# Fewer seven-product chunks in a decoder layer's FFN blocks, and accumulators copied out of PSUM by ScalarE at a block's end

## The chip, the cores and the metric

The kernel runs on one core of a Trainium2 chip. Its time is in device microseconds (us), and lower is better. TensorE (PE in the profile) multiplies, VectorE (DVE) and ScalarE (ACT) work elementwise, GpSimd (POOL) does almost nothing here, and SyncE (SP) issues the weight loads. Each of these engines executes its own instructions in its own fixed order and waits for the others by semaphores.

## The reference: what is computed

One decoder layer over 256 tokens of width 2048, in float32: an FFN, a mixer (attention and a recurrent branch), and a second FFN, each followed by a layer norm. The change concerns the two FFNs, which have the same form:

```python
D_MODEL = 2048
SEQ = 256
D_FF = (8 * D_MODEL // 3 + 255) // 256 * 256      # 5632

def swiglu(h, w_in, w_out):
    a, b = jnp.split(h @ w_in, 2, axis=-1)
    return (jax.nn.silu(a) * b) @ w_out

h = layer_norm(DN_ALPHA * h + 0.5 * swiglu(h, ffn1_w_in[l], ffn1_w_out[l]), ln1_g[l], ln1_b[l])
...
h = layer_norm(DN_ALPHA * h + 0.5 * swiglu(h, ffn2_w_in[l], ffn2_w_out[l]), ln3_g[l], ln3_b[l])
```

## The kernel before

**Precision.** A float32 operand is split into a high part (`h`, rounded to fp32r) and a low part (`l`, the rest), and a product is made of three matmuls, high by high, high by low, low by high (`three`, L563 to L566). The activations are the stationary operand and the weights the moving one. So every weight piece that comes from memory has to be split on the chip: ScalarE copies it to the high part `wh` (L192), VectorE subtracts that from the piece to get the low part `wl` (L193).

**Blocks.** `w_in` is worked through in 22 blocks. A block makes 256 columns of `a` and 256 columns of `b` for both halves of the tokens (t = 0 and 1, 128 each), summed over K = 2048. K is cut into four chunks of 512 (four rows of 128).

- A *plain* chunk consists of two pieces of 128x1024, `c` in the plan. Each piece brings 12 matmuls of 512 columns (2 rows x 2 token halves x 3), 24 in a chunk. They accumulate into two PSUM banks, `c[0]` for the first token half and `c[1]` for the second, each with `a` in its left 256 columns and `b` in its right ones. These banks come from the pool `mm`, which has two buffers (`CB`).
- A *seven-product* chunk replaces the eight half-size products of a 2x2 by 2x2 block product with seven (Winograd's form). It has four pieces named by the products they feed: `p1q3` and `q5p7` and `q4p6` with 1024 columns, `p2` with 512. Each product is 6 matmuls of 256 columns, 42 in a chunk. The products p1, p6, p7 and q5 gather in two banks `e` of the pool `bp` (four buffers); the others go straight into `c`. VectorE must first form sums of weights: `ws` (L165, 128x1024) and two of 128x512 (L169, L172).

**Filling work.** The product with `w_out` does not wait for all blocks. A block's plan holds pieces `o` (`fill`), each of which is 12 matmuls of 512 columns into two banks of the pool `ob`, made of gated results of an earlier group of blocks.

**The order on TensorE** is written out by hand by `block_plan(fast, fills, lead)`: `fast` chunks go by seven products, `fills` pieces `o` are spread between, `lead` of them at the very start. Before the change the plans are, after the first two blocks: two pairs of `block_plan(2, 2, 0)` and `block_plan(3, 2)`, then sixteen late blocks `block_plan(3, 4)`. Word for word, the plans that matter run:

```
(2, 2, 0)  c0 p1q3 p2 c2 q5p7 o q4p6 c8 p1q3 p2 o q5p7 c10 q4p6
(3, 2)     o o c0 p1q3 p2 q5p7 q4p6 p1q3 p2 c2 q5p7 q4p6 p1q3 p2 q5p7 q4p6
(2, 2)     o o c0 p1q3 p2 c2 q5p7 q4p6 c8 p1q3 p2 c10 q5p7 q4p6
(3, 4)     o o c0 p1q3 p2 q5p7 o q4p6 p1q3 p2 c2 q5p7 q4p6 p1q3 o p2 q5p7 q4p6
(2, 4)     o o c0 p1q3 p2 o q5p7 c2 q4p6 o p1q3 p2 c8 q5p7 c10 q4p6
```

A block with `lead` 0 thus begins at once with a plain piece, and the others have two pieces `o` ahead of it.

**Pieces ahead.** `Weights.unit` hands out a piece and, before that, has the piece four places ahead split (`AHEAD` = 4) and the one eight places ahead loaded. The split parts `wh` and `wl` have five buffers each (`HL_BUFS`), so a piece can only be split once TensorE has finished the piece five places before it.

**The gate.** When a block is done, `gate` (L853 on) combines `c` and `e` into `a` and `b`, applies Silu to `a` and multiplies. For a block with seven-product chunks ScalarE copies p1 (L859), VectorE makes six operations (L860, L861, L862, twice L865, and the product L871) and ScalarE the Silu (L866). The two operations L865 are the only readers of the banks `c`, and they stand behind the other sums. Seven pieces later (four for the last block) TensorE transposes the result (L877) and it is split again (L689, L690). The order of ScalarE's and VectorE's instructions is not written by hand: a scheduler places the gate's operations between the splits of the next pieces.

**After the last block** `out_product` multiplies the last group of gated results with the rest of `w_out`; its first bank comes from the same pool `mm`.

Of the kernel before, what the change touches and what calls it, by code (L numbers as in the profile page):

```python
# [8 lines left out]
F32 = mybir.dt.float32  # L9
F32R = mybir.dt.float32r  # L10
I32 = mybir.dt.int32
AF = mybir.ActivationFunctionType
OP = mybir.AluOpType
AX = mybir.AxisListType.X

P = 128
S = 256
# [36 lines left out]
Z_BUFS = 1  # L54
# [12 lines left out]
def block_plan(fast, fills, lead=2):  # L67

    chunks = {0: (), 2: (1, 3), 3: (1, 2, 3)}[fast]
    plain = [("c", k) for q in range(4) if q not in chunks for k in (4 * q, 4 * q + 2)]
    forms = [(f, q) for q in chunks for f in FORMS]
    rest = ["o"] * fills
    plan = [(rest.pop(), 0) for _ in range(min(lead, fills))] + [plain.pop(0)]
    slow = []
    while plain or rest:
        for which in (rest, plain) if lead else (plain, rest):
            if which:  # L80
                p = which.pop(0)
                slow.append((p, 0) if p == "o" else p)
    if not forms:
        return plan + slow
    step = len(forms) / (len(slow) + 1)
    n = 0
    for i, f in enumerate(forms):
        plan.append(f)
        if len(slow) > n and i + 1 >= (n + 1) * step:
            plan.append(slow[n])  # L90
            n += 1
    return plan


def layer_plans(first):
    return ([block_plan(0, 0), block_plan(first, 0)] + [block_plan(2, 2, 0), block_plan(3, 2)] * 2
            + [block_plan(3, 4)] * 16)


FILLS = [(g, nb, 2 * p) for g, (b0, b1) in enumerate(SEGS[:-1]) for nb in range(4) for p in range(b1 - b0)]  # L100
# [161 lines left out]
def tile_layer(ctx, tc, x_fm, x_tm, pos, f1a, f1o, wA, wki, wB, lru, wab, wrb, wo, f2a, f2o,  # L262
# [5 lines left out]
    V, A, T, G = nc.vector, nc.scalar, nc.tensor, nc.gpsimd  # L268
    count = [0]

    def name(s):
        count[0] += 1
        return f"{s}{count[0]}"
# [65 lines left out]
    for i in range(NR + LAG):  # L339
        if i < NR:  # L340
            plain([wB[RX + i], wB[RG + i]])
        if i >= LAG:
            g, c = divmod(i - LAG, TPG)
# [8 lines left out]
    W = Weights(nc, pool, pieces, bg.step)  # L352
# [498 lines left out]
    def ffn(x, forms, ln, plans):  # L851
        def gate(c, e, g, i, lag):

            z = W.fast_pool.tile([P, 4 * S], F32, name=name("z"), tag="z", bufs=Z_BUFS)
            z4 = z.rearrange("p (j c) -> p j c", j=4)
            a, b = z4[:, 0:4:2], z4[:, 1:4:2]
            if e:
                p1, p6, p7, q5 = e[0][:, :S], e[0][:, S:], e[1][:, :S], e[1][:, S:]
                A.activation(z4[:, 0], p1, AF.Copy)  # L859
                V.tensor_tensor(z4[:, 1], z4[:, 0], p6, op=OP.add)  # L860
                V.tensor_tensor(z4[:, 2], z4[:, 1], p7, op=OP.add)  # L861
                V.tensor_tensor(b, q5[:, None, :].to_broadcast([P, 2, S]), z4[:, 1:3], op=OP.subtract)  # L862
                for t in range(2):
                    zt = z[:, t * 512:(t + 1) * 512]
                    V.tensor_tensor(zt, zt, c[t], op=OP.add)  # L865
                A.activation(a, a, AF.Silu)  # L866
            else:
                for t in range(2):
                    A.activation(z4[:, 2 * t], c[t][:, :S], AF.Silu)
                    A.activation(z4[:, 2 * t + 1], c[t][:, S:], AF.Copy)  # L870
            V.tensor_tensor(a, a, b, op=OP.mult)  # L871
            for _ in range(lag):
                yield
            ps = BP()
            for k in range(2):
                for t in range(2):
                    T.transpose(ps[:, k * S + t * P:k * S + (t + 1) * P], z[:, t * 512 + k * P:t * 512 + (k + 1) * P], ident)  # L877
            for k in range(2):
                hl = UHL("g")
                split(hl, ps[:, k * S:(k + 1) * S])  # L880
                g[i + k] = hl

        g = [[None] * (2 * (b1 - b0)) for b0, b1 in SEGS]
        fills = deque(FILLS)
        open_ps = []

        def seed():
            s, nb, _ = fills[0]
            open_ps[:] = OB(), OB()

        def fill():
            if not open_ps:
                seed()
            s, nb, k0 = fills.popleft()
            for k in (k0, k0 + 1):
                w = W.unit(512)
                for t in range(2):
                    tokens(open_ps[t], g[s][k], t, w, k == 0, k == len(g[s]) - 1)
            if k0 + 2 == len(g[s]):
                for t in range(2):  # L900
                    y_add(open_ps, nb, False, t)
                if fills:
                    seed()

        for s, (b0, b1) in enumerate(SEGS):
            for n in range(b0, b1):
                c, e = blockF(x, forms, plans[n], fill)
                task = gate(c, e, g[s], 2 * (n - b0), LAG_T[n == NBK - 1])
                next(task)
                bg.add("gate", task)  # L910
        new_stats()
        ln.prepare()
        if not ln.last:
            bg.add("main", later(consts(), W.last.ins))
        out_product(g[-1], ln)
# [239 lines left out]
    for j in range(NR + LAG):  # L1155
# [14 lines left out]
        if j >= LAG:  # L1170
            i = j - LAG
            g, c = divmod(i, TPG)
# [6 lines left out]
            r, t = T1(), T1()  # L1179
# [114 lines left out]
```

## Time and profile before

| | |
|---|---|
| time, median of 3 runs (lowest to highest) | 2427.51 us (2427.35 to 2430.88) |
| the profiled execution: its time | 2428.93 us |
| the profiled execution: its span, first to last instruction | 2427.0 us |
| mean granted TensorE clock | 0.987 |
| busy time of PE, DVE, ACT | 2313.7 us, 2038.9 us, 1410.3 us |
| first FFN's late blocks | about 181 to 686 us |
| second FFN's late blocks | about 1857 to 2362 us |

A row of the time line reads: start, duration, engine, line, operation, output and inputs by the names in the program, shapes, and in brackets how long the engine had sat idle before and what ended that. Matmuls overlap: one of 512 columns is shown as 0.38 us long, though the next begins after some 0.22 us. So an idle time, which is counted from a shown end, is a little shorter than the gap in the stream. A wait for several semaphores is put down to the one that came last by the profile, which need not be the one that the instruction needed.

### The profile page before, as it was taken

To read this page: it belongs to the slowest core of one execution; us is meant where nothing else is said; L and a number is where in the kernel's file an instruction comes from. 1 tells how busy PE (TensorE), PEld (TensorE's weight loads), DVE (VectorE), ACT (ScalarE), POOL (GpSimd) and SP (SyncE) were. 2 spreads that over 40 slices of the span, in tenths; PEclk is the share of its full clock that TensorE was granted. 3 is DMA by queue.
4 is the path that set the end of the run, shared out by engine and by line. 5 is a ranking of instruction groups with operands and counts; after the bars stand their busy time and mean duration, and the time that the engine had idled before them with its cause. 6 is when DMAs were issued, how large, how long until landed. Compare 5 with 4: busy or idle time off the path is not lost.

```text
span 2427.0 us, 37550 instructions
## 1 busy us (share of the span) xinstructions
PE 2313.7 (95%) x14592; PEld 2104.2 (87%) x14592; DVE 2038.9 (84%) x2835; ACT 1410.3 (58%) x1931; POOL 25.9 (1%) x58
## 2 busy tenths in 40 slices
PE   7889999999989999999999999999989999999997
PEld 6788888888878888888999988888878888888886
DVE  7889999999987776655788875666989999999996
ACT  6555655655646555544688874444755655655652
POOL 0000000000000000000000000000000000000001
PEclk9999999999999999999999999999999999999998
DMA  7445555555556554455555555556645555556563
GB/s 285 167 171 195 208 198 197 193 193 194 197 178 213 180 177 156 148 183 189 176 190 183 182 198 185 187 192 194 213 172 203 193 189 199 197 207 222 208 215 111
DMA packets 112770, 463.41 MB, mean 191 GB/s; under 512 B 12720, under 2 KB 12720, under 8 KB 97488
## 3 DMA queue, kind: packets, MB, share of 16 engines
q1 hardware_dynamic: 110592, 454.61, 53.6%
q0 software_dynamic: 2000, 6.41, 1.0%
q8 instruction: 114, 1.87, 0.3%
q14 instruction: 64, 0.52, 0.1%
HBM read 458.87 MB, written 2.10 MB: 190 GB/s over the span
## 4 chain that ended last, share of the span: by engine, by line
PE 83%; DVE 8%; issue 5%; ACT 3%; DMA 1%; POOL 0%; DVEq 0%; SPq 0%; ACTq 0%; POOLq 0%
PE mm L564 8%; PE mm L566 8%; PE mm L565 8%; PE ob L564 6%; PE ob L566 6%; PE ob L565 6%; PE mm L553 5%; PE ob L553 5%; PE bp L566 4%; PE bp L565 4%; PE bp L564 4%; DVE wl L193 3%; PE mm L554 3%; PE ob L554 3%; ACT wh L192 2%
## 5 line engine op out<-in xcount | busy, mean ns | idle before, releaser
L193 DVE TENSOR_TENSOR wl<-raw,wh 128x1024 fp32r<-128x1024 f32 (+3 forms) x630 | 752.7, 1202 | 300.8 <-ACT wh L192 300.3
L192 ACT ACTIVATE wh<-raw 128x1024 fp32r<-128x1024 f32 (+3 forms) x630 | 652.8, 1045 | 502.7 <-issue 146.3
L192 ACT ACTIVATE wh<-rf 128x1024 fp32r<-128x1024 f32 x354 | 320.5, 916 | 181.6 <-PE mm L566 143.9
L193 DVE TENSOR_TENSOR wl<-rf,wh 128x1024 fp32r<-128x1024 f32 x354 | 365.9, 1041 | 10.6 <-ACT wh L192 7.0
L564 PE MATMUL ob<-wh,g 128*128 128x512 f32 x640 | 246.6, 385 | 1.0 <-ACT g L689 1.0
L566 PE MATMUL ob<-wh,g 128*128 128x512 f32 x640 | 243.2, 380 | 0.6 <-DVE g L690 0.6
L565 PE MATMUL ob<-wl,g 128*128 128x512 f32 x640 | 243.1, 380 | 0.0
L564 PE MATMUL mm<-wh,hs 128*128 128x512 f32 (+1 forms) x600 | 207.5, 346 | 30.0 <-ACT wh L192 15.7
L192 ACT ACTIVATE wh<-ws 128x1024 fp32r<-128x1024 f32 x118 | 125.3, 1061 | 146.2 <-issue 62.9
L566 PE MATMUL mm<-wh,hs 128*128 128x512 f32 (+1 forms) x600 | 205.0, 342 | 1.7 <-DVE hs L755 1.4
L565 PE MATMUL mm<-wl,hs 128*128 128x512 f32 (+1 forms) x600 | 204.6, 341 | 0.0
L564 PE MATMUL mm<-wh,xs 128*128 128x256 f32 (+1 forms) x464 | 156.6, 338 | 46.2 <-ACT wh L192 24.5
L565 PE MATMUL bp<-wl,sh 128*128 128x256 f32 x708 | 195.1, 276 | 1.6 <-DVE wl L193 1.6
L566 PE MATMUL bp<-wh,sl 128*128 128x256 f32 x708 | 194.7, 275 | 0.0
L564 PE MATMUL bp<-wh,sh 128*128 128x256 f32 x708 | 194.6, 275 | 0.0
L564 PEld LDWEIGHTS mm<-wh,hs 128*128 128x128 f32 x600 | 114.6, 191 | 48.3 <-ACT wh L192 22.6
L565 PE MATMUL mm<-wl,xs 128*128 128x256 f32 (+1 forms) x464 | 154.2, 332 | 1.3 <-DVE wl L193 1.3
L193 DVE TENSOR_TENSOR wl<-ws,wh 128x1024 fp32r<-128x1024 f32 x118 | 144.0, 1221 | 13.1 <-ACT wh L192 13.1
L566 PE MATMUL mm<-wh,xs 128*128 128x256 f32 (+1 forms) x464 | 154.2, 332 | 0.0
L165 DVE TENSOR_TENSOR ws<-rf 128x1024 f32<-128x1024 f32 x118 | 143.8, 1219 | 0.0
L564 PEld LDWEIGHTS mm<-wh,xs 128*128 128x128 f32 x464 | 90.4, 195 | 60.6 <-ACT wh L192 30.5
L565 PEld LDWEIGHTS bp<-wl,sh 128*128 128x128 f32 x708 | 135.8, 192 | 3.6 <-DVE wl L193 2.4
(301 smaller groups left out, 5795.3 us busy)
## 6 DMA issues: line engine op xcount, KB each, us to landing
raw<-wB SPq DMA_DIRECT2D x144, 512.0 KB, 3.6
rf<-f1a SPq DMA_DIRECT2D x60, 1024.0 KB, 4.8
rf<-f2a SPq DMA_DIRECT2D x58, 1024.0 KB, 4.9
raw<-f1o SPq DMA_DIRECT2D x88, 512.0 KB, 5.7
raw<-f2o SPq DMA_DIRECT2D x88, 512.0 KB, 5.7
raw<-wA SPq DMA_DIRECT2D x64, 512.0 KB, 3.6
raw<-f2a SPq DMA_DIRECT2D x60, 512.0 KB, 4.9
raw<-f1a SPq DMA_DIRECT2D x56, 512.0 KB, 5.7
```

Of the source, the lines that this page charges most:

```text
L165: v.tensor_tensor(t, b[:, 0:4:3], b[:, 1:2].to_broadcast([P, 2, 2, 256]), op=OP.add)
L192: nc.scalar.activation(hp, src, AF.Copy)
L193: self.last = nc.vector.tensor_tensor(lp, src, hp, op=OP.subtract)
L553: T.matmul(ps, w[0], x.rearrange("p a t -> p (a t)"), start=first, stop=False)
L554: T.matmul(ps[:, :S], w[1], x[:, 0], start=False, stop=last)
L564: T.matmul(ps, xh, h, start=start, stop=False, skip_group_check=seeded)
L565: T.matmul(ps, xh, l, start=False, stop=False, skip_group_check=seeded)
L566: T.matmul(ps, xl, h, start=False, stop=stop, skip_group_check=seeded)
```

## The change

Two edits, in `layer_plans` and in `gate`.

1. The plans. The second block of each early pair goes from `block_plan(3, 2)` to `block_plan(2, 2)`; of the sixteen late blocks every second one goes from `block_plan(3, 4)` to `block_plan(2, 4)`, so that late blocks alternate between three and two seven-product chunks. In each FFN that is 2 + 8 = 10 chunks which become plain.
2. The gate. The tile `z` grows from four to six parts of 256 columns. ScalarE copies each bank `c[t]` to SBUF in one instruction (L860, `a` into part 0 or 2, `b` into part 4 or 5), then p1 (L861). VectorE works on with the copies: L862 to L867 and the product, now L873. The Silu is L868.

```diff
 def layer_plans(first):
-    return ([block_plan(0, 0), block_plan(first, 0)] + [block_plan(2, 2, 0), block_plan(3, 2)] * 2
-            + [block_plan(3, 4)] * 16)
+    return ([block_plan(0, 0), block_plan(first, 0)] + [block_plan(2, 2, 0), block_plan(2, 2)] * 2
+            + [block_plan(3, 4), block_plan(2, 4)] * 8)
...
-            z = W.fast_pool.tile([P, 4 * S], F32, name=name("z"), tag="z", bufs=Z_BUFS)
-            z4 = z.rearrange("p (j c) -> p j c", j=4)
-            a, b = z4[:, 0:4:2], z4[:, 1:4:2]
+            z = W.fast_pool.tile([P, 6 * S], F32, name=name("z"), tag="z", bufs=Z_BUFS)
+            z6 = z.rearrange("p (j c) -> p j c", j=6)
+            a, b = z6[:, 0:4:2], z6[:, 1:4:2]
             if e:
                 p1, p6, p7, q5 = e[0][:, :S], e[0][:, S:], e[1][:, :S], e[1][:, S:]
-                A.activation(z4[:, 0], p1, AF.Copy)
-                V.tensor_tensor(z4[:, 1], z4[:, 0], p6, op=OP.add)
-                V.tensor_tensor(z4[:, 2], z4[:, 1], p7, op=OP.add)
-                V.tensor_tensor(b, q5[:, None, :].to_broadcast([P, 2, S]), z4[:, 1:3], op=OP.subtract)
                 for t in range(2):
-                    zt = z[:, t * 512:(t + 1) * 512]
-                    V.tensor_tensor(zt, zt, c[t], op=OP.add)
+                    A.activation(z6[:, 2 * t:5 + t:4 - t], c[t].rearrange("p (j c) -> p j c", j=2), AF.Copy)
+                A.activation(z6[:, 1], p1, AF.Copy)
+                V.tensor_tensor(z6[:, 0], z6[:, 0], p1, op=OP.add)
+                V.tensor_tensor(z6[:, 1], z6[:, 1], p6, op=OP.add)
+                V.tensor_tensor(z6[:, 3], z6[:, 1], p7, op=OP.add)
+                V.tensor_tensor(z6[:, 2], z6[:, 2], z6[:, 3], op=OP.add)
+                V.tensor_tensor(b, q5[:, None, :].to_broadcast([P, 2, S]), b, op=OP.subtract)
+                V.tensor_tensor(b, b, z6[:, 4:6], op=OP.add)
                 A.activation(a, a, AF.Silu)
```

How the scheduler places the new operations is shown at three places. The numbers behind the names count buffers; `mm` are the banks `c`, `bp` the banks `e`, `raw`, `rf` and `ws` the unsplit pieces, and `wh` with a number is the piece of that number.

On ScalarE, at the end of the first FFN's thirteenth block, a late one (its gate is the tile z173), before. The pieces 208 and 209 are the third and fourth of the following block.

```order
L192 ACTIVATE wh208_4023<-raw208_3954 128x1024
L192 ACTIVATE wh209_4039<-rf209_3973 128x1024
L859 ACTIVATE z173_4057<-bp166_3794 128x256
L192 ACTIVATE wh210_4068<-rf209_3973 128x512
L192 ACTIVATE wh211_4085<-ws209_4041 128x1024
L192 ACTIVATE wh212_4106<-raw212_4021 128x1024
L866 ACTIVATE z173_4057<-z173_4057 128x2x256
```

The same place after; the pieces 198 and 199 are here the third and fourth of the following block.

```order
L192 ACTIVATE wh197_3906<-raw197_3828 128x1024
L192 ACTIVATE wh198_3916<-raw198_3847 128x1024
L860 ACTIVATE z173_3952<-mm164_3667 128x2x256
L192 ACTIVATE wh199_3934<-rf199_3866 128x1024
L860 ACTIVATE z173_3952<-mm165_3668 128x2x256
L861 ACTIVATE z173_3952<-bp166_3687 128x256
L192 ACTIVATE wh200_3964<-rf199_3866 128x512
L192 ACTIVATE wh201_3983<-raw201_3904 128x1024
L868 ACTIVATE z173_3952<-z173_3952 128x2x256
```

The copy of the first bank now stands ahead of the split of the next block's fourth piece, that of the second bank right behind it, and the Silu two splits after the copy of p1 where it was three.

On VectorE, the same gate before.

```order
L860 TENSOR_TENSOR z173_4057<-z173_4057,bp166_3794 128x256
L169 TENSOR_TENSOR rf209_3973<-ws209_4041,rf209_3973 128x2x256
L861 TENSOR_TENSOR z173_4057<-z173_4057,bp167_3795 128x256
L193 TENSOR_TENSOR wl210_4069<-rf209_3973,wh210_4068 128x512
L862 TENSOR_TENSOR z173_4057<-bp167_3795,z173_4057 128x2x256
L172 TENSOR_TENSOR rf209_3973<-rf209_3973 128x2x256
L865 TENSOR_TENSOR z173_4057<-z173_4057,mm164_3774 128x512
L865 TENSOR_TENSOR z173_4057<-z173_4057,mm165_3775 128x512
L193 TENSOR_TENSOR wl211_4086<-ws209_4041,wh211_4085 128x1024
L871 TENSOR_TENSOR z173_4057<-z173_4057 128x2x256
```

And after.

```order
L862 TENSOR_TENSOR z173_3952<-z173_3952,bp166_3687 128x256
L863 TENSOR_TENSOR z173_3952<-z173_3952,bp166_3687 128x256
L169 TENSOR_TENSOR rf199_3866<-ws199_3936,rf199_3866 128x2x256
L864 TENSOR_TENSOR z173_3952<-z173_3952,bp167_3688 128x256
L193 TENSOR_TENSOR wl200_3965<-rf199_3866,wh200_3964 128x512
L865 TENSOR_TENSOR z173_3952<-z173_3952 128x256
L193 TENSOR_TENSOR wl201_3984<-raw201_3904,wh201_3983 128x1024
L866 TENSOR_TENSOR z173_3952<-bp167_3688,z173_3952 128x2x256
L172 TENSOR_TENSOR rf199_3866<-rf199_3866 128x2x256
L867 TENSOR_TENSOR z173_3952<-z173_3952 128x2x256
L193 TENSOR_TENSOR wl202_4004<-ws199_3936,wh202_4003 128x1024
L873 TENSOR_TENSOR z173_3952<-z173_3952 128x2x256
```

No operation of VectorE reads a bank `mm` any more, and the gate's operations lie between three splits where they lay between two.

On ScalarE at the end of the first FFN's fourth block (gate z83), behind which a block with `lead` 0 begins, before.

```order
L192 ACTIVATE wh52_1171<-rf51_1087 128x512
L192 ACTIVATE wh53_1190<-raw53_1123 128x1024
L859 ACTIVATE z83_1206<-bp78_980 128x256
L192 ACTIVATE wh54_1219<-ws51_1161 128x1024
L866 ACTIVATE z83_1206<-z83_1206 128x2x256
L192 ACTIVATE wh55_1238<-raw55_1157 128x1024
```

And after.

```order
L860 ACTIVATE z83_1184<-mm76_969 128x2x256
L192 ACTIVATE wh50_1149<-rf49_1066 128x512
L192 ACTIVATE wh51_1168<-raw51_1101 128x1024
L860 ACTIVATE z83_1184<-mm77_970 128x2x256
L861 ACTIVATE z83_1184<-bp78_988 128x256
L192 ACTIVATE wh52_1200<-ws49_1133 128x1024
L192 ACTIVATE wh53_1219<-raw53_1129 128x1024
L192 ACTIVATE wh54_1237<-rf49_1066 128x1024
L868 ACTIVATE z83_1184<-z83_1184 128x2x256
L192 ACTIVATE wh55_1247<-raw55_1166 128x1024
```

The Silu, which needs results of VectorE, stood one split behind the copy of p1 and now stands three behind it.

More of the change, by code (lines that the diff above doesn't have):

```diff
@@ L868, in gate @@
                 for t in range(2):
-                    A.activation(z4[:, 2 * t], c[t][:, :S], AF.Silu)
-                    A.activation(z4[:, 2 * t + 1], c[t][:, S:], AF.Copy)
+                    A.activation(z6[:, 2 * t], c[t][:, :S], AF.Silu)
+                    A.activation(z6[:, 2 * t + 1], c[t][:, S:], AF.Copy)
             V.tensor_tensor(a, a, b, op=OP.mult)
```

## Prediction

> **What bounds the kernel now.** I read the page first, for the busy time by slices.
>
> ```profile
> PE 2313.7 (95%) x14592; PEld 2104.2 (87%) x14592; DVE 2038.9 (84%) x2835; ACT 1410.3 (58%) x1931; POOL 25.9 (1%) x58
> PE   7889999999989999999999999999989999999997
> DVE  7889999999987776655788875666989999999996
> ```
>
> TensorE looks full everywhere; VectorE is full in the first and last third alone, which are the two FFNs. The windows tell the two apart there: thirteen late blocks of the first FFN, from one gate to another (start and end are the two copies of p1 below), and a stretch of two early blocks.
>
> ```profile
> 246.28:654.60 408.32, 393.71 (x2627) 364.07 (x2626) 402.45 (x482) 243.98 (x287) 0.00 (x0) 1.00 0.54 201
> 66.12:118.38 52.26, 51.92 (x338) 48.09 (x338) 44.53 (x54) 29.48 (x36) 0.00 (x0) 0.97 0.45 162
> 246.28 0.39 ACT L859 ACTIVATE z<-bp 128x256 f32<-128x256 f32 x1 [0.28 <-PE bp L566]
> 654.60 0.38 ACT L859 ACTIVATE z<-bp 128x256 f32<-128x256 f32 x1 [0.28 <-PE bp L566]
> ```
>
> A late block takes 408.32 / 13 = 31.41 us. VectorE is busy for 402.45 / 13 = 30.96 us of it (98.6%), TensorE for 30.29. So in the late blocks VectorE sets the pace. In the early stretch VectorE is busy for only 85% and TensorE hardly waits (0.34 us in 52).
>
> Where TensorE loses its time is seen in its time line and VectorE's, around one block's end.
>
> ```profile
> 403.35 0.38 PE L565 MATMUL ob<-wl,g 128*128 128x512 f32 x1
> 408.10 0.38 PE L566 MATMUL ob<-wh,g 128*128 128x512 f32 x1
> 409.62 0.45 PE L564 MATMUL mm<-wh,xs 128*128 128x512 f32 x1 [1.14 <-ACT wh L192]
> 409.91 0.38 PE L565 MATMUL mm<-wl,xs 128*128 128x512 f32 x1
> 408.79 1.28 DVE L865 TENSOR_TENSOR z<-z,mm 128x512 f32<-128x512 f32 x2
> 408.52 1.06 ACT L192 ACTIVATE wh<-raw 128x1024 fp32r<-128x1024 f32 x1 [1.53 <-PE ob L566]
> ```
>
> The profile blames a split, but that is the wrong name: in ScalarE's order the split at 408.52 is wh212, and the first plain piece that TensorE starts at 409.62 is wh208, four splits earlier. What ends just before 409.62 is the first of the two operations L865 (begun at 408.79, some 0.6 us each), which frees the bank `c[0]`. TensorE waits for VectorE's gate. The other such waits:
>
> ```profile
> 66.12 0.77 PE L564 MATMUL mm<-wh,xs 128*128 128x512 f32 x1 [7.52 <-DVE z L865]
> 127.68 0.77 PE L564 MATMUL mm<-wh,xs 128*128 128x512 f32 x1 [9.03 <-DVE z L865]
> 188.05 0.45 PE L564 MATMUL mm<-wh,xs 128*128 128x512 f32 x1 [2.72 <-DVE z L865]
> 221.14 0.45 PE L564 MATMUL mm<-wh,xs 128*128 128x512 f32 x1 [1.12 <-ACT wh L192]
> 690.74 0.76 PE L564 MATMUL mm<-wh,g 128*128 128x512 f32 x1 [4.78 <-DVE z L865]
> 1803.23 0.77 PE L564 MATMUL mm<-wh,hs 128*128 128x512 f32 x1 [9.03 <-DVE z L865]
> 1863.79 0.45 PE L564 MATMUL mm<-wh,hs 128*128 128x512 f32 x1 [2.71 <-DVE z L865]
> 2366.59 0.77 PE L564 MATMUL mm<-wh,g 128*128 128x512 f32 x1 [3.46 <-DVE z L865]
> ```
>
> The row at 221.14 stands for 30: fifteen in each FFN, one a late block, 1.11 to 1.27 us each. The long ones stand where a block with `lead` 0 follows, and behind the last block.
>
> **The change part by part.**
>
> *Matmuls: a loss.* The page counts the seven-product chunks by their loads: 60 and 58. After the change there are 50 and 48.
>
> ```profile
> rf<-f1a SPq DMA_DIRECT2D x60, 1024.0 KB, 4.8
> rf<-f2a SPq DMA_DIRECT2D x58, 1024.0 KB, 4.9
> 412.28 0.27 PE L564 MATMUL bp<-wh,xs 128*128 128x256 f32 x1
> 415.52 0.28 PE L566 MATMUL bp<-wh,sl 128*128 128x256 f32 x1
> ```
>
> From 403.35 to 408.10 lie 22 steps of 512 columns, 0.216 us each; from 412.28 to 415.52 lie 29 steps of 256, 0.1117 us each. A plain chunk costs 24 x 0.216 = 5.18 us, one by seven products 42 x 0.1117 = 4.69 us. Twenty chunks cost TensorE 20 x 0.49 = **9.8 us** more. [...]
>
> *VectorE: relief.*
>
> ```profile
> 402.32 2.35 DVE L193 TENSOR_TENSOR wl<-raw,wh 128x1024 fp32r<-128x1024 f32 x2
> 404.59 1.22 DVE L193 TENSOR_TENSOR wl<-rf,wh 128x1024 fp32r<-128x1024 f32 x1
> 405.73 0.41 DVE L860 TENSOR_TENSOR z<-z,bp 128x256 f32<-128x256 f32 x1
> 406.06 0.68 DVE L169 TENSOR_TENSOR rf<-ws,rf 128x512 f32<-128x512 f32 x1
> 406.66 0.41 DVE L861 TENSOR_TENSOR z<-z,bp 128x256 f32<-128x256 f32 x1
> ```
>
> From start to start an operation of 1024 columns takes 1.135 us, of 512 0.60, of 256 0.33. A seven-product chunk has four of 1024 (`ws` and three `wl`) and three of 512, 6.34 us; a plain one two of 1024, 2.27. That frees 4.07 us a chunk, 81 us in all. The gate hardly changes: two of 256 and four of 512 before (3.06 us), four and three after (3.12).
>
> *Loads.* A plain chunk comes in two loads of 512 KB in place of one of 1024, the same bytes, and SyncE issues them ahead as before; with a DMA share of 0.54 in the late stage I cost that at nothing. Loads that came late would be seen as ScalarE waiting for DMA.
>
> *The new balance.* Without its wait a late block is 30.04 us on TensorE: 31.41 less 1.37, which is the gap of 1.52 us from 408.10 to 409.62 less a step of 0.216, plus 0.07 for the slow first step. A light block, with two chunks, is 30.53. VectorE needs 30.96 + 0.06 in a heavy block and 4.07 less in a light one, 57.97 for a pair against TensorE's 60.57: 95.7%. So VectorE has room over a pair and TensorE should set the pace. In a heavy block alone VectorE is still 0.98 us over.
>
> *The banks.* The copies on ScalarE are new. A copy of a full bank has its price in the trace.
>
> ```profile
> L977 ACT ACTIVATE stg<-mm x8: 597/597/599, 766.2 to 944.3; 128x512 f32<-128x512 f32 x8
> 128.23 0.63 ACT L866 ACTIVATE z<-z 128x512 f32<-128x512 f32 x1 [7.75 <-DVE z L865]
> ```
>
> Two copies add 1.2 us a block, 49 us over 41 blocks; ScalarE is busy for 244 of 408 us, so that fits. The copy of `c[1]` waits for the block's last matmul. Behind it in ScalarE's queue stand the copy of p1, the splits of the fifth and sixth next piece, and the Silu. With two pieces `o` ahead (2 x 12 x 0.216 = 5.2 us) the banks are free long before they are wanted. With `lead` 0 the plain piece wants `c[0]` at once, which is copied before the block's last matmul, and `c[1]` three steps (0.65 us) later: I allow 0.7 us there, between 0 and the 2.4 us that two splits ahead of the copy would make.
>
> *The sum.* A wait is counted from the shown end of a matmul, so each hides another 0.16 us (0.38 less 0.216). A long one also slows what comes after:
>
> ```profile
> 66.67 0.63 PE L565 MATMUL mm<-wl,xs 128*128 128x512 f32 x1
> 69.17 0.38 PE L565 MATMUL mm<-wl,xs 128*128 128x512 f32 x1
> 180.00:200.00 20.00, 17.28 (x95) 15.10 (x94) 18.24 (x23) 9.59 (x14) 0.00 (x0) 0.91 0.39 143
> ```
>
> From 66.12 to 69.17 lie seven steps, 3.05 us in place of 1.51: 1.54 us lost. The window around the 2.72 us wait shows the same, a granted clock of 0.91 over 20 us.
>
> - Thirty late waits: 30 x 1.37 = 41.1 us.
> - Three long ones ahead of `lead` 0: 7.52 + 9.03 + 9.03, and 3 x 1.70, less 3 x 0.7 that stay: 28.6 us.
> - Those ahead of the first late block: 2.72 + 2.71 + 2 x 1.70 = 8.8 us.
> - Those behind the last block: 4.78 + 3.46 + 2 x 1.70 = 11.6 us. The gated result is still needed three pieces on, and the gate then has less time; I take 10.
> - Dearer matmuls: -9.8 us.
> - New short waits, where a heavy block outruns VectorE: between 0 (as at 85%) and 16 x 0.98 = 16 us (the light block's slack is of no use). I take 0.2 us a late block, 6 us, near the row of the early stretch, since four pieces are split ahead: -6.
>
> Together 88.5 - 15.8 = **72.7 us**. The profiled execution took 2428.93, which leaves 2356.2; the median of the runs is 1.4 us below it. So I forecast **2355 us**. The shares above belong to one FFN stage each, so nothing in the mixer moves.
>
> **The rivals.**
>
> *VectorE still sets the heavy block's pace* (and part of the long waits goes on as waits for splits). For: 30.96 us of work against 30.04, and with five buffers it can't work far ahead. Against: two early blocks ran with 0.34 us of waits, heavy one included. Then only the light blocks gain, 16 x 0.88 = 14 us in place of 41.1 - 7.8 - 6 = 27, and of 38 us of long waits a third stays: 13 + 13 less, about 2381.
>
> *The copies do nothing*: the name in the profile is right, TensorE waits in late blocks for a split, and frees no time when the banks come free. Then the 41.1 us stay and the rest goes: 2396. Against it stands the order of the splits, told above.
>
> *ScalarE holds up TensorE, and the kernel is slower.* ScalarE's queue is in order: the row at 128.23 shows it standing 7.75 us at the Silu, with splits queued behind. Now it also stands at the copies, at each of 41 block ends, and behind a `lead` 0 block three splits come ahead of the Silu. If the splits behind come late by more than the four pieces ahead cover, TensorE waits once a block. It decides from 72.7 / 41 = 1.8 us a block; at 2.72 us, the shortest wait that is seen to lower the clock, with 1.70 behind it, it would be 41 x 4.4 = 181 us and the time about 2535; at 2.4 us, without the clock, 98 us and 2453. Against it: the pieces 200 to 202 behind the copies are wanted 9 us after the block's end (two `o`, `c0`, `p1q3`). [...]
>
> **How the numbers follow.** My forecast, from 2340 (every wait gone, none new, and the waits for the last gated result too) to 2370, has 0.73; the heavy block's pace, 2370 to 2392, 0.16; the copies doing nothing 0.05; ScalarE 0.04; 0.02 for no change, if gains and losses cancel. The range 2340 to 2380 leaves out the last three and about half of the second, some 2 in 10. Of 0.2%, which is what a measurement here tells from no change, both likely cases are far on the faster side: faster 0.94, same 0.02, slower 0.04.
>
> ```profile
> ACT z L866 <- DVE z L865: 58.7, 41, 7.7
> ```
>
> **What would show it.** Right: late blocks alternate at about 30.1 and 30.6 us; TensorE's rows at their first plain piece carry no wait; the rows of 7.5 to 9 us are under 1 us; VectorE is busy for about 96% in the late stage; ScalarE's waits at the Silu, 58.7 us in all in the row above, shrink, since they no longer include VectorE's reads of the banks. Wrong: waits of TensorE for splits (L192, L193) of about 1 us in each heavy block, a late stage that VectorE still fills by 98%, or ScalarE idle at L860 with TensorE idle after it.

## The result and the profile after

The changed kernel takes 2344.45 us (median of 4 runs, 2342.45 to 2347.84), the kernel before beside it 2427.43. The ratio is 0.9656, with a 95% interval from 0.964 to 0.9673. The forecast was 2355 us in a range from 2340 to 2380.

The page of the profile after, in the lines that answer to those of before:

```profile
span 2341.9 us, 36807 instructions
PE 2303.4 (98%) x14232; PEld 2096.1 (90%) x14232; DVE 1965.3 (84%) x2776; ACT 1415.3 (60%) x1973; POOL 25.6 (1%) x58
DVE  7999999999987786555788875665999999999996
```

By slices hardly anything changed for VectorE; it is still nine tenths busy in the FFNs. The windows tell more; here are six pairs of late blocks, from one copy of p1 to another.

```profile
220.75:584.27 363.52, 363.52 (x2318) 336.23 (x2317) 350.42 (x427) 225.87 (x277) 0.00 (x0) 1.00 0.58 208
```

The first matmuls of three blocks in a row, from TensorE's time line, enclose a light block (two seven-product chunks) and then a heavy one (three).

```profile
250.50 0.38 PE L564 MATMUL ob<-wh,g 128*128 128x512 f32 x1
281.03 0.38 PE L564 MATMUL ob<-wh,g 128*128 128x512 f32 x1
311.08 0.38 PE L564 MATMUL ob<-wh,g 128*128 128x512 f32 x1
```

TensorE is busy for all of 363.52 us, VectorE for 96.4%. Light and heavy blocks alternate at 30.53 and 30.05 us, and a pair takes 363.52 / 6 = 60.59 us where it took 62.82. Of TensorE's waits for the banks `c` none is left. Ahead of the first copy of p1 two waits for splits stand as they did before (0.60 and 0.56 us, at 50.26 and 53.20). From there to the end of each FFN, all idle times of TensorE over 0.4 us lie behind the last block and are for its gated result; at the end of that block itself (644.44) TensorE goes on at once:

```profile
644.44 0.28 PE L566 MATMUL bp<-wh,sl 128*128 128x256 f32 x1
644.55 0.38 PE L564 MATMUL mm<-wh,g 128*128 128x512 f32 x1
653.90 0.48 PE L564 MATMUL mm<-wh,g 128*128 128x512 f32 x1 [0.98 <-ACT g L689]
655.91 0.79 PE L566 MATMUL mm<-wh,g 128*128 128x512 f32 x1 [1.30 <-DVE g L690]
2288.79 0.48 PE L564 MATMUL ob<-wh,g 128*128 128x512 f32 x1 [0.98 <-ACT g L689]
2290.11 0.48 PE L566 MATMUL ob<-wh,g 128*128 128x512 f32 x1 [0.62 <-DVE g L690]
```

Where a block with `lead` 0 follows, TensorE stood 7.5 to 9 us. After, the time lines of ScalarE and TensorE at the first such place read:

```profile
58.20 0.58 ACT L860 ACTIVATE z<-mm 128x512 f32<-128x512 f32 x1
58.24 0.28 PE L566 MATMUL bp<-wh,sl 128*128 128x256 f32 x1
58.35 0.38 PE L564 MATMUL mm<-wh,xs 128*128 128x512 f32 x1
59.01 0.38 PE L564 MATMUL mm<-wh,xs 128*128 128x512 f32 x1
```

The copy of `c[1]` begins at 58.20, while TensorE still works on the last product of the old block, and is done at 58.78; the new block writes that bank from 59.01 on. To compare runs I use the two stretches from the first copy of p1 to the last of each FFN, which leave out the start and the mixer (which differ by up to 5 us between runs with the same work there). Of before and of after:

```profile
58.63:686.00 627.37, 590.58 (x3908) 545.56 (x3908) 603.25 (x723) 363.89 (x429) 0.00 (x0) 0.99 0.52 193
1768.26:2361.87 593.61, 563.94 (x3749) 521.04 (x3748) 576.85 (x692) 348.30 (x410) 4.30 (x8) 0.99 0.54 198
```

```profile
58.68:644.85 586.17, 586.17 (x3730) 541.70 (x3729) 566.86 (x694) 366.43 (x449) 0.00 (x0) 1.00 0.58 207
1718.17:2279.74 561.57, 561.24 (x3570) 518.60 (x3569) 540.57 (x661) 349.22 (x429) 4.26 (x8) 1.00 0.58 210
```

Of the 85.1 us by which the span is shorter (2427.0 to 2341.9), 41.2 and 32.0 lie in these stretches, 8.9 between them and 3.0 behind the second, both of which hold the waits behind a last block.

### The profile page after: what moved, and what is told of

Read it like the earlier page. It is cut to its first block, busy times and chain, and to the rows that moved or that the text cites. A ratio compares the mean times of both kernels' runs of the same rounds, so it can differ in the third digit from the quotient of the medians.

```text
span 2341.9 us, 36807 instructions
## 1 busy us (share of the span) xinstructions
PE 2303.4 (98%) x14232; PEld 2096.1 (90%) x14232; DVE 1965.3 (84%) x2776; ACT 1415.3 (60%) x1973; POOL 25.6 (1%) x58
## 4 chain that ended last, share of the span: by engine, by line
PE 87%; DVE 5%; issue 5%; ACT 2%; DMA 1%; POOL 0%; DVEq 0%; SPq 0%; ACTq 0%; POOLq 0%
PE mm L566 9%; PE mm L564 9%; PE mm L565 9%; PE ob L564 7%; PE ob L566 7%; PE ob L565 7%; PE mm L553 6%; PE ob L553 5%; PE bp L566 3%; PE bp L565 3%; PE bp L564 3%; PE mm L554 3%; PE ob L554 3%; DVE wl L193 3%; PE mm L1148 2%
## 5 line engine op out<-in xcount | busy, mean ns | idle before, releaser
L193 DVE TENSOR_TENSOR wl<-raw,wh 128x1024 fp32r<-128x1024 f32 (+3 forms) x670 | 802.2, 1202 | 277.0 <-ACT wh L192 276.1
L192 ACT ACTIVATE wh<-raw 128x1024 fp32r<-128x1024 f32 (+3 forms) x670 | 697.8, 1047 | 507.3 <-PE mm L566 142.6
L192 ACT ACTIVATE wh<-rf 128x1024 fp32r<-128x1024 f32 (+1 forms) x294 | 267.9, 919 | 132.1 <-PE mm L566 78.7
L193 DVE TENSOR_TENSOR wl<-rf,wh 128x1024 fp32r<-128x1024 f32 (+1 forms) x294 | 301.6, 1039 | 11.2 <-ACT wh L192 9.6
L564 PE MATMUL mm<-wh,xs 128*128 128x512 f32 (+1 forms) x504 | 172.6, 343 | 9.9 <-ACT wh L192 6.8
L565 PE MATMUL mm<-wl,xs 128*128 128x512 f32 (+1 forms) x504 | 172.1, 341 | 1.3 <-DVE wl L193 1.3
L566 PE MATMUL mm<-wh,xs 128*128 128x512 f32 (+1 forms) x504 | 171.5, 340 | 0.0
L566 PEld LDWEIGHTS ob<-wh,g 128*128 128x128 f32 x640 | 121.2, 189 | 18.3 <-DVE g L690 1.0
L564 PEld LDWEIGHTS ob<-wh,g 128*128 128x128 f32 x640 | 121.7, 190 | 16.5 <-ACT g L689 1.4
L566 PEld LDWEIGHTS mm<-wh,hs 128*128 128x128 f32 x640 | 121.5, 190 | 15.5 <-DVE hs L755 3.0
L565 PEld LDWEIGHTS ob<-wl,g 128*128 128x128 f32 x640 | 121.5, 190 | 14.3
L564 PEld LDWEIGHTS mm<-wh,hs 128*128 128x128 f32 x640 | 121.6, 190 | 13.9 <-ACT z L872 2.0
L565 PEld LDWEIGHTS mm<-wl,hs 128*128 128x128 f32 x640 | 121.6, 190 | 11.3
```

Source lines behind the costliest of these rows:

```text
L192: nc.scalar.activation(hp, src, AF.Copy)
L193: self.last = nc.vector.tensor_tensor(lp, src, hp, op=OP.subtract)
L564: T.matmul(ps, xh, h, start=start, stop=False, skip_group_check=seeded)
L565: T.matmul(ps, xh, l, start=False, stop=False, skip_group_check=seeded)
L566: T.matmul(ps, xl, h, start=False, stop=stop, skip_group_check=seeded)
```

## The experiments

The ratio of each kernel is to the kernel before, timed beside it (2427.4 to 2429.4 us). The last column is the sum of the two FFN stretches in the profiled execution.

| kernel | median us | ratio to before, 95% interval | FFN stretches us |
|---|---|---|---|
| before | 2427.43 | 1 | 1221.0 |
| after | 2344.45 | 0.9656 (0.9640 to 0.9673) | 1147.7 |
| plans alone | 2440.61 | 1.0047 (1.0035 to 1.0060) | 1236.5 |
| gate alone | 2374.63 | 0.9776 (0.9763 to 0.9790) | 1177.7 |
| after, copies made twice | 2347.16 | 0.9663 (0.9650 to 0.9676) | 1154.2 |
| after, split three ahead | 2357.06 | 0.9706 (0.9693 to 0.9719) | 1167.2 |
| plans alone, `lead` 3 | 2384.46 | 0.9816 (0.9799 to 0.9832) | 1178.8 |
| after, all late blocks light | 2350.48 | 0.9672 (0.9659 to 0.9685) | 1154.8 |
| after, two of three heavy | 2350.82 | 0.9678 (0.9665 to 0.9692) | 1157.0 |
| after, three of four heavy | 2351.79 | 0.9679 (0.9666 to 0.9692) | 1158.1 |
| after, late blocks with `lead` 0 | 2342.74 | 0.9645 (0.9632 to 0.9658) | 1151.2 |
| after, last transposes earlier | 2338.63 | 0.9627 (0.9614 to 0.9641) | 1147.5 |

### The plans alone

```diff
 def layer_plans(first):
-    return ([block_plan(0, 0), block_plan(first, 0)] + [block_plan(2, 2, 0), block_plan(3, 2)] * 2
-            + [block_plan(3, 4)] * 16)
+    return ([block_plan(0, 0), block_plan(first, 0)] + [block_plan(2, 2, 0), block_plan(2, 2)] * 2
+            + [block_plan(3, 4), block_plan(2, 4)] * 8)
```

> The plans of after with the gate of before. My theory: the banks came free late because VectorE was behind with everything; with the plans it has room, and a gate then ends about 5.2 us after p1's copy (as ahead of 98.43 in before's trace, where nothing was queued), which two pieces o (5.2 us) just cover. So the 30 late waits of 1.37 us go, all but 0.3 us of each, and what stays are the waits ahead of lead 0 and behind the last block, some 5 us each and five in all, with 1.5 us of slow clock behind the longer ones. That is 25 to 40 us over after: 2369 to 2385. Rival one, the copies are what freed TensorE: the late waits stay at about 1 us or more each, and with the dearer matmuls the time is 2405 or more. Rival two, VectorE's load is all: within 5 us of after.

It took 2440.61 us: slower than before by 0.5%, far outside what I expected. Only the first rival, with 2405 or more, takes it in, and it had waits of about 1 us in each block. I had thought that a gate ends in time as soon as VectorE has room over a pair. The time lines of VectorE, then of TensorE and ScalarE, at the end of a heavy block show why it does not:

```profile
395.79 1.28 DVE L699 SCALAR_TENSOR_TENSOR y<-ob,y 128x512 f32<-128x512 f32 x2
396.99 2.35 DVE L193 TENSOR_TENSOR wl<-raw,wh 128x1024 fp32r<-128x1024 f32 x2
399.25 1.22 DVE L193 TENSOR_TENSOR wl<-rf,wh 128x1024 fp32r<-128x1024 f32 x1
400.39 0.41 DVE L860 TENSOR_TENSOR z<-z,bp 128x256 f32<-128x256 f32 x1
...
402.86 1.21 DVE L193 TENSOR_TENSOR wl<-raw,wh 128x1024 fp32r<-128x1024 f32 x1
403.99 1.27 DVE L865 TENSOR_TENSOR z<-z,mm 128x512 f32<-128x512 f32 x2
```

```profile
397.39 0.38 PE L564 MATMUL ob<-wh,g 128*128 128x512 f32 x1
397.60 0.38 ACT L859 ACTIVATE z<-bp 128x256 f32<-128x256 f32 x1 [0.27 <-PE bp L566]
404.81 0.73 PE L564 MATMUL mm<-wh,xs 128*128 128x512 f32 x1 [2.07 <-DVE z L865]
```

And windows of this kernel: one around that wait, one of 10 us behind each of two such waits (the one before it, at 341.92, and it), and one over seven pairs of blocks. The granted clock is the third number from the end:

```profile
403.00:409.00 6.00, 4.19 (x12) 3.43 (x13) 5.74 (x7) 1.47 (x2) 0.00 (x0) 0.72 0.61 220
341.72:351.92 10.20, 10.00 (x63) 9.21 (x64) 9.62 (x12) 5.69 (x7) 0.00 (x0) 1.00 0.48 134
404.61:414.81 10.20, 10.00 (x52) 8.84 (x53) 8.23 (x10) 4.51 (x5) 0.00 (x0) 0.83 0.37 116
214.45:663.58 449.13, 434.19 (x2703) 397.63 (x2703) 411.28 (x484) 252.46 (x294) 0.00 (x0) 0.98 0.56 197
```

The block ends at 397.39. VectorE, without a pause, first makes its outstanding sums and three splits and reaches the gate at 400.39, 3.0 us late; between its first operation there and the first L865 stand five more, two of them splits for the next block (the dots leave four out). The bank is free some 7.3 us after the block's end, and two pieces `o` cover 5.2. The wait comes once a pair, not in each block, but behind this one the granted clock is down (0.72 in the window around it, 0.83 over 10 us), which it was not behind the waits of 1.12 us of before (1.00 over thirteen blocks). It does not follow each time: behind the wait at 341.92, of 2.06 us, the clock is 1.00. Seven pairs take 449.13 us, 64.16 each, 1.3 us more than before and 3.6 more than TensorE's 60.57. The wait with its two small parts is 2.3 of that. The other 1.3 is a mean: two of the seven pairs take 62.9 us, with no slow clock, and five take 64.6 to 64.8. So the relief of VectorE alone buys nothing here, and the dearer matmuls are paid for as well.

### The gate alone

The gate of after, the plans of before (the first diff the other way round).

> The gate of after with the plans of before. My theory: VectorE still has 31.0 us of work in each of 32 late blocks, so they stay at 31.0 to 31.4 us against 30.3 on average in after, 23 to 36 us; waits for banks turn into waits for splits. In the early pairs two heavy blocks of 28.5 us of VectorE work stay, which costs another 5 to 10 us. Ten chunks an FFN are cheaper for TensorE, which is of no use here. 2372 to 2390. Rival, the copies are what freed TensorE: late blocks of 30.1 us, no wait, and with 9.8 us less of matmuls about 2335. VectorE's busy share in the late stage tells: 98% or more by my theory.

It took 2374.63 us, as expected. A window over thirteen late blocks, and TensorE's time line at three waits:

```profile
226.47:629.00 402.53, 392.77 (x2621) 365.29 (x2619) 401.59 (x495) 249.24 (x312) 0.00 (x0) 1.00 0.55 204
```

```profile
206.18 0.66 PE L879 MATMUL bp<-ident,z 128*128 128x128 f32 x4 [0.74 <-DVE z L873]
474.12 0.45 PE L564 MATMUL ob<-wh,g 128*128 128x512 f32 x1 [0.72 <-ACT wh L192]
505.13 0.45 PE L564 MATMUL ob<-wh,g 128*128 128x512 f32 x1 [0.73 <-DVE y L699]
```

VectorE is busy for 99.8% and sets the pace, 402.53 / 13 = 31.0 us a block. In the late blocks the banks `mm` are not waited for any more; TensorE waits 0.73 us a block elsewhere, for a bank `ob` that VectorE adds up or for a transpose (the row at 474.12 names a split, that at 505.13, the same matmul a block later, names the sum). The long waits ahead of a block are gone: where `lead` is 0, two are left for ScalarE's copies, 1.06 and 0.51 us. That is most of the 54 us. The plans need the gate, and the gate is worth more with them: it saves 54 us with the old plans and 96 with the new ones, while the plans cost 12 us with the old gate and save 30 with the new.

### Three pieces of cover

Late blocks of the kernel with the plans alone, begun with three pieces `o`:

```diff
-            + [block_plan(3, 4), block_plan(2, 4)] * 8)
+            + [block_plan(3, 4, 3), block_plan(2, 4, 3)] * 8)
```

> The plans of after with the gate of before, and late blocks that begin with three pieces o in place of two. My theory, mended after the run with the plans alone: VectorE has room over a pair, but at a heavy block's end it is some 2.4 us behind, and the operations L865 stand 3 to 4 us further down its queue between splits; so the banks come free 7.2 us after the block's end, 2 us after the two pieces o are through, and a wait of that size lowers the clock besides. A third o makes the cover 7.8 us: the late waits go, some 16 x 3.6 = 58 us, and only the waits ahead of lead 0 and behind the last block stay (five, some 35 us with the clock): 2378 to 2395. Rival: VectorE's order, not the cover, is what is wrong, and the wait moves along with the bank or to a split: 2415 or more.

It took 2384.46 us, 56 less than with two. TensorE's time line has two waits for L865 left in the first FFN's late blocks, where there were eight of over 2 us, and the long ones where no cover was added:

```profile
67.31 0.77 PE L564 MATMUL mm<-wh,xs 128*128 128x512 f32 x1 [7.52 <-DVE z L865]
369.54 0.45 PE L564 MATMUL mm<-wh,xs 128*128 128x512 f32 x1 [0.92 <-DVE z L865]
431.01 0.45 PE L564 MATMUL mm<-wh,xs 128*128 128x512 f32 x1 [0.36 <-DVE z L865]
672.23 0.77 PE L564 MATMUL mm<-wh,g 128*128 128x512 f32 x1 [4.45 <-DVE z L865]
```

So the loss in the late blocks with the plans alone was the time at which a bank comes free against the work that covers it. The two waits that are left stand behind waits of VectorE for a weight load, 2.50 and 1.96 us long, at 362.10 and 423.57. What this kernel still loses on after lies for the most part at the long waits ahead of `lead` 0 (7.52, 5.53 and 5.76 us) and behind the last blocks (4.45 and 3.13).

The order of VectorE's reads was not tested. With the plans alone VectorE reaches the gate 3.0 us after a heavy block's end; were its two reads of the banks `c`, 0.6 us each, the first thing there, the banks would be free some 4.2 us after the end, inside the cover of 5.2. That is an estimate from the rows above. So it is not shown how much of what the gate saves in the late blocks needs ScalarE, and how much only an earlier read.

### No cover

After, with the late blocks begun like the first ones of an early pair:

```diff
-            + [block_plan(3, 4), block_plan(2, 4)] * 8)
+            + [block_plan(3, 4, 0), block_plan(2, 4, 0)] * 8)
```

> After, with lead 0 in all late blocks: a plain piece into the banks c stands right behind the block before, with no piece o to cover the gate. My theory: the copies free the banks within half a microsecond of need (c[1] is last written six matmuls before a block's end), so the cover is not wanted any more: no wait at the first plain piece, 2343 to 2350. Rival, the copies only moved the banks' release ahead by some microseconds and still live off the two pieces o: 0.5 us or more at each of 32 blocks, 2360 or more; with a wait of 2 us and the clock behind it 2400.

It took 2342.74 us, by the intervals not told from after, and TensorE's time line shows no wait over 0.25 us in either stage of late blocks. Its FFN stretches are 3.5 us longer: a heavy block takes 30.29 us in place of 30.05, with a short gap ahead of the transposes and none at the first plain piece. With the banks read by ScalarE the pieces `o` at a block's start are not needed to cover the gate.

### ScalarE's copies made twice

```diff
                 for t in range(2):
-                    A.activation(z6[:, 2 * t:5 + t:4 - t], c[t].rearrange("p (j c) -> p j c", j=2), AF.Copy)
+                    for _ in range(2):
+                        A.activation(z6[:, 2 * t:5 + t:4 - t], c[t].rearrange("p (j c) -> p j c", j=2), AF.Copy)
```

> After, with each copy of a bank c made twice, which takes ScalarE 1.2 us more a block, 41 blocks, 49 us. My theory: ScalarE has room and the pieces behind are split four ahead, so TensorE waits only ahead of lead 0, for the second copy of c[1], 0.6 us each or 2 us in all: 2343 to 2348. Rival, ScalarE's queue is near to holding up TensorE: a wait in each block of 1 us or so, 41 us more, about 2385.

2347.16 us; by the intervals not told from after. The FFN stretches are 6.5 us longer, somewhat more than expected. Three waits appear for the second copy of `c[1]` where `lead` is 0, and four of about 0.7 us at other places. From TensorE's time line, with one row of VectorE's:

```profile
59.58 0.48 PE L564 MATMUL mm<-wh,xs 128*128 128x512 f32 x1 [0.87 <-ACT z L861]
110.99 0.48 PE L564 MATMUL mm<-wh,xs 128*128 128x512 f32 x1 [0.42 <-ACT z L861]
584.51 1.23 DVE L165 TENSOR_TENSOR ws<-rf 128x1024 f32<-128x1024 f32 x1 [3.52 <-DMA rf<-f1a]
617.57 0.45 PE L564 MATMUL ob<-wh,g 128*128 128x512 f32 x1 [0.69 <-DVE y L699]
```

All four come 13 to 33 us behind a wait of VectorE for a weight load of 2.8 to 3.5 us, of which the row at 584.51 is one; whether the further copies made the loads late was not followed. ScalarE's queue does not hold up TensorE in each block: 49 us of further copies cost 3 to 6 us.

### Split three ahead

```diff
-HL_BUFS = 5
-AHEAD = 4
-LOADS = 4
+HL_BUFS = 4
+AHEAD = 3
+LOADS = 5
```

> After, with pieces split three ahead in place of four (four buffers in place of five), loads at the same distance. My theory: the four pieces ahead are what lets a heavy block, in which VectorE is 0.98 us over, borrow from the light one, and hides the gate; with three, a piece of a seven-product chunk has only 3.4 to 4 us from the freeing of its buffer to its use, in which ScalarE and VectorE need 2.2 us for it and VectorE up to 2.3 us for sums besides. Waits of TensorE for splits come back, 0.3 to 1 us in each of 98 such chunks: 2375 to 2440. Rival, look-ahead plays no part and VectorE's room over a pair is all: within 5 us of after.

2357.06 us: slower than after, but by 13 us and not by 30 to 95. Waits for splits come back once a pair in the late stage, 0.34 to 0.62 us each, and four of 0.95 to 1.44 us besides, two of which come 11 and 14 us behind a wait of VectorE for a load of 3.16 us; not in each chunk. From TensorE's time line:

```profile
189.89 0.48 PE L565 MATMUL ob<-wl,g 128*128 128x512 f32 x1 [0.62 <-DVE wl L193]
```

I had counted each chunk by itself; my reading, which no run tests further, is that the pieces `o` and `c` between them give back what a chunk takes. With the fourth piece ahead, in after, no wait of TensorE for a split is over 0.25 us between the first copy of p1 and the last in either FFN.

### How many chunks

Three mixes of late blocks, with the gate of after: all light; heavy, heavy, light; heavy, heavy, heavy, light.

```diff
-            + [block_plan(3, 4), block_plan(2, 4)] * 8)
+            + [block_plan(2, 4)] * 16)
...
+            + [block_plan(3, 4), block_plan(3, 4), block_plan(2, 4)] * 5 + [block_plan(3, 4)])
...
+            + [block_plan(3, 4), block_plan(3, 4), block_plan(3, 4), block_plan(2, 4)] * 4)
```

> The gate of after, and all sixteen late blocks of each FFN with two chunks by seven products. My theory: TensorE sets the pace in after, so sixteen more plain chunks cost 16 x 0.49 = 7.8 us and VectorE's share falls to 88%, which is of no use: 2350 to 2354. Rival, VectorE still holds up something in heavy blocks that the waits do not show: no slower than after, 2345 or less.

> The gate of after, late blocks in the order heavy, heavy, light, five times, and one heavy: six chunks fewer are plain. My theory: VectorE needs 89.0 us in three blocks against TensorE's 90.6 (98%), so TensorE still sets the pace and 6 x 0.49 = 2.9 us are gained, 2340 to 2343, if the second heavy block's backlog (2 x 0.98 us) stays within the four pieces ahead. Rival, the second heavy block in a row waits about 1 us as all of them do with the gate alone: ten such blocks, 2347 to 2352.

> The gate of after, late blocks heavy, heavy, heavy, light: eight chunks fewer are plain. VectorE needs 120.0 us in four blocks against 120.65 of TensorE (99.5%). My theory: at this share VectorE's small idle times (0.4 us a block) make it the bound in the second and third heavy block; 3.9 us gained on matmuls and 0.7 us lost in each of 16 blocks: 2346 to 2354. Rival, TensorE still sets the pace: 2339 to 2342.

They took 2350.48, 2350.82 and 2351.79 us. The medians lie 6 to 7 us above after's, at the edge of what the intervals tell; the FFN stretches are longer by 7.1, 9.3 and 10.4 us. All light is as expected: sixteen plain chunks more cost 16 x 0.49 = 7.8 us, and room on VectorE is of no use. For two of three heavy the rival's time was right and mine was not. But its cause, a wait at each second heavy block in a row, is not what the trace shows. The ten groups of three blocks should take 90.64 us each on TensorE. Six of them take 0.1 to 0.3 us more. The other four lose 1.6 to 3.8 us, and each of these begins where VectorE has just waited 2.0 to 4.2 us for a weight load. Of that kernel, two rows of VectorE's time line, each followed by the next wait of TensorE for a sum, and the window in which the second of the loads was due:

```profile
336.68 1.23 DVE L165 TENSOR_TENSOR ws<-rf 128x1024 f32<-128x1024 f32 x1 [2.02 <-DMA rf<-f1a]
369.85 0.45 PE L564 MATMUL ob<-wh,g 128*128 128x512 f32 x1 [0.34 <-DVE y L699]
2162.45 1.23 DVE L165 TENSOR_TENSOR ws<-rf 128x1024 f32<-128x1024 f32 x1 [4.16 <-DMA rf<-f2a]
2195.61 0.45 PE L564 MATMUL ob<-wh,g 128*128 128x512 f32 x1 [0.33 <-DVE y L699]
2158.00:2162.40 4.40, 4.40 (x31) 4.08 (x30) 0.29 (x1) 2.50 (x3) 0.00 (x0) 1.00 1.03 428
```

In that window the DMA engines are busy throughout (the last number but one, 1.03); the load took 9.4 us from issue to landing, where the median is 5.6. After has such waits of VectorE too (2.17 and 1.61 us in the second FFN), but they cost TensorE only 0.5 and 0.3 us. So a late load was not made up for in this kernel, where VectorE needs 98% of TensorE's time by the estimate above and was busy for 97.7% of the window from 217.00 to 643.70 and 96.6% of that from 1850.00 to 2288.00; whether the order of the blocks makes loads late was not tested. With three heavy blocks in a row, groups of four take 121.7 to 122.0 us where no load came over 1 us late, against TensorE's 120.69. So there 1.0 to 1.3 us are lost without a late load, and the time is as expected. Of the mixes tried, one heavy to one light has the lowest median.

### The waits that are left

After, with the last block's transposes one piece earlier:

```diff
-LAG_T = (7, 4)
+LAG_T = (7, 3)
```

> After, with the last block's transposes one piece earlier (three pieces after the gate in place of four), for the only waits of over 0.6 us that TensorE has left in the FFNs, 0.98 and 1.30 us behind the first FFN's last block and 0.98 and 0.62 behind the second's, with slow matmuls after the first. My theory: the gate of a last block ends 5 to 6 us after the block, a little behind the earlier place, so TensorE waits some 0.5 to 1 us there and no longer later: 1 to 5 us faster, 2340 to 2344. Rival: the wait only moves, and the time stays within 2 us of after.

2338.63 us, the fastest of all, though its interval (0.9614 to 0.9641) still touches after's (0.9640 to 0.9673). TensorE now waits once behind each last block, for the gate's product, and no longer for its split result:

```profile
649.87 0.66 PE L879 MATMUL bp<-ident,z 128*128 128x128 f32 x4 [1.78 <-DVE z L873]
2282.08 0.66 PE L879 MATMUL bp<-ident,z 128*128 128x128 f32 x4 [1.75 <-DVE z L873]
```

The two are longer than the 0.5 to 1 us that I had allowed, and yet the time is below the 2340 to 2344 us that I had expected. Of the 6.5 us between the spans of the two profiled executions (2341.9 and 2335.4), 4.5 lie outside the FFN stretches in the parts that hold the waits behind a last block, and 1.8 ahead of the first copy of p1, where the two kernels do not differ. Behind the first FFN's wait the granted clock now stays at 1.00, where in after it was 0.83 over the 10 us from 653.90, behind the waits of 0.98 and 1.30 us. But with no cover it stays at 1.00 behind the same two waits as well (0.98 and 1.32 us), so the clock's part of the gain need not come from the edit.

## Why the prediction was right

**What bounds the kernel.** Right, and so was the reading of the wrongly named wait: with the gate alone TensorE does not wait at the first plain piece of a late block any more, which it would if a split were late there, and with the plans alone the profile names L865 itself at that place. That VectorE sets the pace of a late block shows in the gate alone, where it is busy for 99.8% and a block takes its 31.0 us.

**Matmuls.** 9.8 us for twenty chunks; sixteen more in the all-light kernel cost 7.1 by the stretches against 7.8 by the same price.

**The late waits and the new balance.** A pair was forecast at 60.57 us for TensorE and came out at 60.59, heavy and light blocks at 30.04 and 30.53 and came out at 30.05 and 30.53; VectorE's share at 95.7%, measured 96.4%. ScalarE's waits at the Silu shrank as foretold, from 58.7 us:

```profile
ACT z L868 <- DVE z L865: 35.3, 25, 2.6
```

**Terms that were too careful.** The forecast fell 10.6 us short by the medians and 12.3 by the profiled executions, from which its sum was taken. Three allowances make 9.7 of that. (1) 2.1 us that should stay ahead of `lead` 0: nothing stays. I had the copy of `c[1]` wait for the block's last matmul, but a block's last piece writes `c[1]` first and p6 after it, six matmuls or 0.67 us. The copy starts as soon as ScalarE is through with a split, 0.15 us before the block ends, and is done 0.23 us before TensorE writes the bank, at each of the three places. That margin is thin, and that it is not negative is luck as far as the prediction goes; copies made twice use it up. (2) 1.6 us behind the last block: none stays, TensorE goes on at 644.55 at once and the later waits are no longer than before. (3) 6 us of short waits in heavy blocks: none appear at one heavy to one light. The runs with three heavy blocks in a row and with three pieces ahead show where they begin. Apart from these allowances, each FFN stretch gained about 1.2 us more than the terms that lie in it; short waits for splits of before (0.34 to 0.58 us) that after does not have lie there, and it was not taken further apart.

**Loads at nothing.** For the time this held, but not for the loads themselves: the median from issue to landing of the 1024 KB loads went from 4.8 to 5.7 us, and it is mostly VectorE, not ScalarE as I had it, that waits for late ones, four times in the FFNs by 0.4 to 2.2 us, where before it did not wait for any over 0.3 us. At this mix it costs TensorE under 1 us in all.

**The rivals.** *VectorE still sets the heavy block's pace*: not at this mix, but it is what the gate alone does, and three heavy blocks in a row. *The copies do nothing*: fell. *ScalarE holds up TensorE*: fell by the time and by the doubled copies.

**What the prediction did not see.** It added up the two edits' effects as one sum and told neither what each does alone, nor that one of them alone costs. Its reason for the long waits, a VectorE that is behind because it has too much to do, is half of it. After the change VectorE is about as late at a heavy block's end as with the plans alone: the next block begins at 250.50, and VectorE's first operation of the gate at 253.32.

```profile
249.92 2.35 DVE L193 TENSOR_TENSOR wl<-raw,wh 128x1024 fp32r<-128x1024 f32 x2
252.19 1.22 DVE L193 TENSOR_TENSOR wl<-rf,wh 128x1024 fp32r<-128x1024 f32 x1
253.32 0.41 DVE L862 TENSOR_TENSOR z<-z,bp 128x256 f32<-128x256 f32 x1
```

It no longer matters, because the first thing that TensorE needs of it is the gated result: VectorE has that done at 260.61, and the transposes begin at 262.87. That is the gate's part; the plans' part is that VectorE catches up in the light block: at its end, 281.03, the gate's first operation begins 1.10 us behind, at 282.13, where it was 2.82 us at 250.50.

## What to carry to other kernels

VectorE, with a full queue, also released a bank that TensorE needs, and relief of the queue was not enough: with the plans alone VectorE was busy for 91.6% of seven pairs (411.28 of 449.13 us), and yet it reached the gate 3.0 us after a heavy block's end, and the bank came free some 7.3 us after it. In such a case have the buffer released early, here by ScalarE, which is busy for 62% of the six pairs of after where VectorE is for 96.4%, and only then trade the bound engine's time for the busy one's. Test two edits of one change apart, since here one alone loses 12 us and is worth 30 beside the other. And leave the busy engine some room: with one heavy block to one light, waits of VectorE of 2.17 and 1.61 us for a load cost TensorE 0.5 and 0.3 us; with two to one, waits of 2.0 to 4.2 us cost 1.6 to 3.8.

## What the runs showed that was not expected

With the plans alone the granted clock came down after most waits of 2.1 to 2.7 us: in the late stages it was 0.83 over the next 10 us after thirteen of sixteen, and 1.00 after the other three. In before it did not come down after waits of 1.1 us (1.00 over the 10 us from 221.14). In after it did behind the two waits of 0.98 and 1.30 us (0.83 over the 10 us from 653.90), and in the kernel with no cover not behind the same two (1.00). So in these runs the length of a wait does not decide by itself; what does was not found. With the plans alone, one wait of 2.1 to 2.7 us a pair was dearer than the two of some 1.12 us of before, 3.6 us a pair against 2 x 1.37 us.

ScalarE gained waits that cost nothing, for the split of the gated result:

```profile
ACT g L689 <- DVE g L690: 75.3, 43, 3.4
```

It had 6.7 us of them before; no wait of TensorE in the late stage goes with it.
